# Attention scores of a hybrid decoder layer: two maps of a head by pairs of 64-row matmuls

## The chip, the cores and the metric

The kernel runs on one core of one Trainium2 chip. A core has five engines that run side by side, each with its own queue of instructions: TensorE (PE, matrix products; PEld is its loading of the stationary operand), VectorE (DVE), ScalarE (ACT), GpSimd (POOL) and SyncE (SP, which here issues DMAs). Matrix products land in PSUM, a small memory of 128 partitions in banks of 512 float32 values; everything else lies in SBUF, also with 128 partitions. The metric is device time in microseconds for one execution, lower is better. All times are of the kernel as a whole unless a stretch is named.

## What is computed

One decoder layer on 1024 tokens of width 1024, batch 1, in float32. One RMS norm feeds one input projection. Its columns go to two groups of heads that mix the tokens in parallel: four heads of differential attention, and four heads of a gated delta rule (a chunked recurrence). The outputs are joined, projected, added to the input, and followed by an MLP with squared ReLU (hidden width 4096). The part that the change touches is the attention:

```python
da_q = rms_norm(da_q.reshape(B, S, DA_HEADS, 2, DA_QK_DIM), q_norm_w[l])   # 4 heads, 2 maps, 64 dims
da_k = rms_norm(da_k.reshape(B, S, DA_HEADS, 2, DA_QK_DIM), k_norm_w[l])
...
s = jnp.einsum('bqhcd,bkhcd->bhcqk', qb, k, preferred_element_type=jnp.float32) * scale
s = jnp.where(causal, s, jnp.finfo(jnp.float32).min)
p = jax.nn.softmax(s, axis=-1)
a = p[:, :, 0] - lam * p[:, :, 1]
return jnp.einsum('bhqk,bkhe->bqhe', a.astype(v.dtype), v)
```

For each head there are two maps. Each map has queries and keys of 64 dimensions; the two softmax maps are subtracted with a learned factor and the difference is applied to values of 128 dimensions.

## The kernel before

**Precision.** Products that need more than one rounded operand are made with the type fp32r: a float32 matrix is split into a high part (rounded to fp32r) and a low part (the rest), and the products high·high, high·low and low·high are added up in PSUM. The projections do so with three matmuls for each block of 128 (lines 1089 to 1091 for the attention's projection, 267 to 269 for the delta rule's, 1389 to 1391 for the output projection).

**Queries and keys.** `da_units` projects blocks of 256 columns (two heads of two maps) for each of eight blocks of 128 tokens, and normalises them. `da_turns` transposes such a block with two matmuls against the identity (lines 1050 and 1051), writes high and low part into the tile `qa` of `[128, 2, 256]` (lines 1054 and 1055), and stores it in device memory as `qk_d`. On the host the columns of the units of q and k are reordered before the launch (map before head), so that one transposed block of 128 rows holds one map of two heads.

**Scores.** `scores` walks through 32 units: a head h and a block of 128 queries tb. The unit looks at n = 128·(tb+1) keys. Where n is over 512, the keys are cut into two pieces of pl = n/2, because a matmul writes at most one bank. `load_head` brings the keys of a head: for each of the two maps a tile `KS0` or `KS1` with the 64 dimensions of the high part in the upper half of the partitions and those of the low part in the lower half. `load_q` brings the queries of a unit twice: in `qa` as high over low, in `qb` as low over high. A matmul of all 128 rows with `qa` gives high·high + low·low, one with `qb` gives low·high + high·low (lines 1216 and 1217). So a map takes two matmuls for each piece, and a unit four or eight.

**Softmax.** A map's scores lie in one PSUM tile of two banks. One instruction on VectorE (line 1227) negates the scores, adds the causal mask, writes them to SBUF as `pexp`, and keeps the row minimum; ScalarE then takes the exponential with that minimum as bias and sums the rows (line 1228). When both maps are done, VectorE combines them (lines 1236 to 1239).

**Values.** `values` transposes the combined map (line 1261), copies it (line 1263), multiplies it with the values (line 1273), normalises the result and stores it or keeps it for the output projection.

**Order of the work.** A planner, the class `Interleave`, runs generators (`scan`, `da_units`, `da_turns`, `scores`, `values`, `mixed`, `outproj`) and decides in which order their matmuls stand in TensorE's one queue. Each generator says when it may go on; `flow.pe` advances the planner's clock by an estimate of PE time, `flow.chain` estimates when the other engines will have finished, and `flow.hold` keeps a PSUM buffer taken until then. For scores there are two PSUM buffers, `qsc` and `rsc`, which take turns once the delta rule's scan has been emitted. The estimates decide the order; on the chip the engines wait for semaphores. The instructions of the other engines are put in order by the framework's own scheduler. SP's queue carries the loads of `KS`, of the queries, of weights and of rows for the output projection.

Of the kernel before, what the change touches and what calls it, by code (L numbers as in the profile page):

```python
# [9 lines left out]
F32 = mybir.dt.float32  # L10
F32R = mybir.dt.float32r
BF16 = mybir.dt.bfloat16
AF = mybir.ActivationFunctionType
ALU = mybir.AluOpType
# [4 lines left out]
P = 128  # L19
SEQ = 1024  # L20
DM = 1024
KB = DM // P
NT = SEQ // P
HEADS = 4
DQK = 64
# [84 lines left out]
def act(n, accum=False):  # L110
    return "S", 55.0 + 0.83 * n + (93.0 if accum else 0.0)


def vec(n, extra=0.0):
    return "V", 68.0 + 1.045 * n + extra
# [7 lines left out]
def tile_hymba_layer(  # L123
# [6 lines left out]
    nc = tc.nc  # L130
    V, S, G, T = nc.vector, nc.scalar, nc.gpsimd, nc.tensor
# [45 lines left out]
    qk_d = dram.tile([2, 2, NT, P, 2, 2 * P], F32, name="qk_d")  # L177
# [85 lines left out]
    quarters, newest = Quarters(), {}  # L263
# [219 lines left out]
    with tc.manual_schedule(engines={T.engine, V.engine, S.engine, G.engine}):  # L483
# [38 lines left out]
        pools = {3: (pj, "pj"), 4: (ph, "ph"), 5: (pt_, "pt"), 6: (pj, "pj"), 7: (ph, "ph")}  # L522
# [10 lines left out]
        for tb in range(3, NT):  # L533
            for u in range(2):
                nxt, at = spread_at.get((tb, u), (None, 0))
                z[tb, u] = z_mm(tb, u, *pools[tb], nxt, at)
                if nxt is not None:
# [4 lines left out]
                    if nxt in (4, 5):  # L542
                        b = {4: 5, 5: 7}[nxt]
# [73 lines left out]
    u, au, e, w1, lw, d1, z1 = (n32(n) for n in ("gu", "gau", "gte", "gw1", "glw", "gd1", "gz1"))  # L617
# [128 lines left out]
    for h in range(HEADS):  # L746
        for hf in range(2):
            rh, rl = ta("rrh", 1, F32R), ta("rrl", 1, F32R)
            for t, col in ((rh, ggh), (rl, ggl)):
                for c in range(4):  # L750
                    i = cidx(h, 4 * hf + c)
# [26 lines left out]
    for h, hf, y, th in skew(dn_proj(1)):  # L778
# [6 lines left out]
        for c in range(4):  # L785
            i = cidx(h, 4 * hf + c)
# [9 lines left out]
        for c in range(4):  # L796
            i = cidx(h, 4 * hf + c)
            cs = slice(c * P, (c + 1) * P)
# [52 lines left out]
    for h, hf, q2 in skew(dn_proj(0)):  # L851
# [6 lines left out]
        for c in range(4):  # L858
            i = cidx(h, 4 * hf + c)
# [3 lines left out]
        for c in range(4):  # L863
            i = cidx(h, 4 * hf + c)
            cs = slice(c * P, (c + 1) * P)
# [26 lines left out]
    ae = actx.enter_context(tc.tile_pool(name="ae", bufs=4, **right))  # L892
    dctx = ctx.enter_context(ExitStack())
    ap = dctx.enter_context(tc.tile_pool(name="ap", bufs=1, **right))
# [6 lines left out]
    flow = Interleave()  # L901
    MK = 512 + P
    mk = ap.tile([P, MK], BF16, name="mk")
# [7 lines left out]
    pools, T_ops = {}, []  # L911
# [222 lines left out]
    def load_head(h, pool):  # L1134

        KS = []
        for m in range(2):
            k = pool.tile([P, SEQ], F32R, tag=f"KS{m}", name=f"KS{m}")
            for s in range(2):
                nc.sync.dma_start(k[HF[s]].bitcast(F32).rearrange("p (b t) -> p b t", t=P),  # L1140
                                  qk_d[h // 2, 1, :, HF[h % 2], s, m * P:(m + 1) * P].rearrange("b p t -> p b t"))
            KS.append(k)
        return KS

# [3 lines left out]
        return vt  # L1148

    def load_q(h, tb):  # L1150
        qa = ap.tile([P, 2, P], F32R, tag="qa", name="qa", bufs=2)
        qb = ap.tile([P, 2, P], F32R, tag="qb", name="qb", bufs=2)
        for s in range(2):
            src = qk_d[h // 2, 0, tb, HF[h % 2], s, :]
            nc.sync.dma_start(qa[HF[s]].bitcast(F32).rearrange("p m t -> p (m t)"), src)
            newest["SP"] = nc.sync.dma_start(qb[HF[1 - s]].bitcast(F32).rearrange("p m t -> p (m t)"), src)
        return qa, qb

    order = [(0, t) for t in range(NT)] + [(1, t) for t in range(NT)]
    order += [(h, t) for t in reversed(range(NT)) for h in (2, 3)]  # L1160
# [2 lines left out]
    def scores():  # L1163
        heads, npe, nsc = {}, 0, 0
        while state["da"] < 1:
            yield flow.now + 300, None
        yield flow.now + HEAD_T, None
        heads[0] = load_head(0, ap), load_v(0, ap)
        q = load_q(*order[0])
        yield flow.now + 6000, None  # L1170
        for u, (h, tb) in enumerate(order):
            if u >= NT - 3 and 1 not in heads and state["scan"] or h == 1 and 1 not in heads:

                while not state["scan"]:
                    yield flow.now + 300, None
                with tc.issue_after(newest["SP"].ins):
                    heads[1] = load_head(1, pools["a2"]), load_v(1, pools["a2"])
                if h == 1:
                    yield flow.now + 5000, None
            if h == 2 and h not in heads:  # L1180
                while state["turned"] < 3 * NT:
                    yield flow.now + 300, None
                ks = load_head(2, ap), load_head(3, pools["a2"])
                while state["da"] < 2:
                    yield flow.now + 300, None
                q = load_q(h, tb)
                heads[2] = ks[0], load_v(2, ap)
                heads[3] = ks[1], load_v(3, pools["a2"])
                yield state["da_t"] + 2000, None
            if q is None:  # L1190
                q = load_q(h, tb)
                yield flow.now + 3000, None
            while u < 2 * NT and u > 2 + 0.4 * (state["units"] - 3 * NT) and not state["proj"]:

                yield flow.now + 100, None
            while len(ready) > (AHEAD if state["scan"] else 0):
                yield flow.now + 100, None
            KS, vt = heads[h]
            qa, qb = q
            n = (tb + 1) * P  # L1200
            npc = 1 if n <= 512 else 2
            pl = n // npc
            pe, ssum = [], ap.tile([P, 2], F32, tag="ssum", name="ssum", bufs=4)
            mx = ap.tile([P, 2], F32, tag="mx", name="mx", bufs=4)
            for m in range(2):
                nsc += 1
                if state["scan"] and nsc % 2:
                    name, sc = "rsc", pools["rsc"]
                else:
                    name, sc = "qsc", qsc  # L1210
                yield 0, name
                sc = sc.tile([P, 1024], F32, tag="sc", name="ps_sc")
                for pc in range(npc):
                    o = sc[:, 512 * pc:512 * pc + pl]
                    ks = KS[m][:, pc * pl:(pc + 1) * pl]
                    T.matmul(o, qa[:, m, :], ks, start=True, stop=False)
                    T.matmul(o, qb[:, m, :], ks, start=False, stop=True)
                npe += 1
                ep = pools["be"] if state["scan"] and npe % 3 == 0 else ae
                e = ep.tile([P, SEQ], F32, tag="pexp", name="pexp")  # L1220

                scv, ev, mv = sc[:, :n], e[:, :n], mk[:, MK - n:]
                if npc == 2:
                    scv = sc.rearrange("p (a b) -> p a b", b=512)[:, :, :pl]
                    ev = ev.rearrange("p (a b) -> p a b", a=2)
                    mv = bass.AP(mk.tensor, mk.offset, [[MK, P], [MK - pl, 2], [1, pl]])
                V.tensor_tensor_reduce(ev, scv, mv, -1.0, 3.0e38, ALU.add, ALU.min, mx[:, m:m + 1])  # L1227
                S.activation(e[:, :n], e[:, :n], AF.Exp, scale=-1.0, bias=mx[:, m:m + 1],  # L1228
                             accum_out=ssum[:, m:m + 1])
                flow.pe(2 * max(n / 2.4, 110.0))  # L1230
                t = flow.chain(vec(n, 60))
                flow.hold(name, t)
                t = flow.chain(act(n, True), start=t - flow.HOP)
                pe.append(e)
            ri = ap.tile([P, 2], F32, tag="ri", name="ri", bufs=4)
            V.reciprocal(ri, ssum)
            cf = ap.tile([P, 1], F32, tag="cf", name="cf", bufs=4)
            V.scalar_tensor_tensor(cf, ssum[:, 0:1], nlam, ri[:, 1:2], ALU.mult, ALU.mult)
            V.scalar_tensor_tensor(pe[0][:, :n], pe[1][:, :n], cf, pe[0][:, :n], ALU.mult, ALU.add)
            t = flow.chain(vec(10), vec(1, 60), vec(n, 100), start=t - flow.HOP)  # L1240
            if u + 1 < len(order) and order[u + 1][0] // 2 < state["da"]:
                q = load_q(*order[u + 1])
            ready.append((h, tb, pe[0], ri, vt, t))
# [685 lines left out]
def _laid_out(_np, inputs):  # L1929


    w_in, w_out = (_np.asarray(inputs.pop(n))[0].reshape(KB, P, -1).transpose(1, 0, 2) for n in ("w_in", "w_out"))
    w_z = _np.zeros((2, KB // 2, P, 576), w_in.dtype)
    w_z[..., :2 * UC] = w_in[:, :, 3072:].reshape(P, KB // 2, 2, 2, UC).transpose(3, 1, 0, 2, 4).reshape(
        2, KB // 2, P, 2 * UC)
    units = w_in[:, :, :3072].reshape(P, KB, 12, 256).transpose(2, 0, 1, 3).copy()

    units[:4] = units[:4].reshape(4, P, KB, 2, 2, DQK).transpose(0, 1, 2, 4, 3, 5).reshape(4, P, KB, 256)
    halves = w_out.reshape(P, KB, 2, 512).transpose(2, 0, 1, 3)

    x_cols = _np.asarray(inputs["x"])[0].reshape(NT, P, KB, P).transpose(0, 3, 2, 1)
    w1_cols = _np.asarray(inputs.pop("norm1_w"))[0].reshape(KB, P).T
    return dict(inputs, x_cols=x_cols, w1_cols=w1_cols, w_z=w_z, w_units=units, w_halves=halves)
# [24 lines left out]
```

## Time and profile before

| what | value |
|---|---|
| median of 3 runs | 1227.69 us (1225.83 to 1229.32) |
| the profiled execution's own time | 1227.74 us |
| its span | 1226.0 us |
| granted TensorE clock, mean | 0.998 |
| instructions | 18798 |
| PE matmuls | 6743 |
| score matmuls (lines 1216 and 1217) | 192, from 359.5 to 571.3 us |
| DMA packets | 179269, 202.12 MB |

How to read the profile: a line such as `L1216 PE MATMUL ps_sc<-KS,qa 128*128 128x512 f32 x24` names the line of the kernel, the engine, the operation, output and inputs by the program's names, the stationary operand's rows times columns, the size of the moving one, and how many there were. A duration of a matmul includes the pipeline through the array, which overlaps the next matmul; the distance between two starts shows what a matmul costs in a row of them. In the waits view a line reads: who waited, for whom, microseconds in total, times, longest. In the windows view the columns are the stretch, its length, the busy time of PE, PEld, DVE, ACT and POOL with their numbers of instructions, the granted clock, the share of DMA, and GB/s. SPq is the queue in which SP issues DMAs.

### The profile page before, as it was taken

How to read it: one execution, taken by the hardware profiler on the slowest of the kernel's cores; microseconds unless marked ns; L12 is line 12 of the kernel's file. 1: busy time of each engine (PE TensorE's matmuls, PEld its weight loads, DVE VectorE, ACT ScalarE, POOL GpSimd, SP SyncE). 2: the span in 40 equal slices, each digit the busy share in tenths (PEclk: the TensorE clock that was granted, in tenths of full speed). 3: DMA queues.
4: the chain of work that ended last, by engine and by line, in shares of the span. 5: the costliest groups of instructions: out<-in, count | busy, mean ns of one | idle time of the engine just before them, and what ended most of it. 6: DMA issues, size and time to landing. Idle time of an engine off the chain costs nothing.

```text
span 1226.0 us, 18798 instructions
## 1 busy us (share of the span) xinstructions
PE 1208.2 (99%) x6743; PEld 1045.9 (85%) x6743; DVE 836.9 (68%) x1566; ACT 624.0 (51%) x1257; POOL 151.9 (12%) x215
## 2 busy tenths in 40 slices
PE   9999999999998999999999999999999999999998
PEld 7978888899998998888888888888888888888886
DVE  6868797667567667677798554566569755777543
ACT  6588554344355665566766444454563333333330
POOL 2411110035334431002200000000000000000000
PEclk9999999999999999999999999999999999999999
DMA  9334654378748865333628433444479555422301
GB/s 349 105 113 119 169 163 81 84 233 234 249 145 265 244 157 144 79 83 93 204 88 292 155 125 141 165 177 150 154 258 403 214 180 186 150 103 103 137 35 69
DMA packets 179269, 202.12 MB, mean 165 GB/s; under 512 B 63032, under 2 KB 135272, under 8 KB 179176
## 3 DMA queue, kind: packets, MB, share of 16 engines
q1 hardware_dynamic: 174552, 187.28, 48.0%
q0 software_dynamic: 4480, 13.64, 3.0%
q8 instruction: 53, 0.87, 0.3%
q14 instruction: 40, 0.33, 0.1%
q10 hardware_dynamic: 144, 0.00, 0.0%
HBM read 135.86 MB, written 65.01 MB: 164 GB/s over the span
## 4 chain that ended last, share of the span: by engine, by line
PE 91%; ACT 3%; DVE 2%; DMA 2%; SPq 1%; issue 1%; POOL 0%; DVEq 0%; ACTq 0%
PE X L1567 5%; PE X L1565 5%; PE X L1566 5%; PE X L1864 4%; PE X L1863 4%; PE X L1865 4%; PE ps_dn L267 3%; PE ps_qk L1089 3%; PE ps_dn L269 3%; PE ps_dn L268 3%; PE ps_qk L1090 3%; PE ps_qk L1091 3%; PE Y L1567 3%; PE Y L1565 3%; PE Y L1566 3%; PE ps_o L1273 3%
## 5 line engine op out<-in xcount | busy, mean ns | idle before, releaser
L1483 ACT CAST hH<-ur 128x1024 fp32r<-128x1024 f32 x56 | 58.9, 1051 | 173.3 <-PE Y L1864 90.3
L1484 DVE TENSOR_TENSOR hL<-ur,hH 128x1024 fp32r<-128x1024 f32 x56 | 68.4, 1223 | 79.8 <-ACT hH L1483 79.6
L1089 PE MATMUL ps_qk<-wH,hH 128*128 128x256 f32 x384 | 114.5, 298 | 0.7 <-DVE sn L1110 0.7
L1484 DVE TENSOR_TENSOR op<-raw,op 128x1024 fp32r<-128x1024 f32 x48 | 58.7, 1224 | 74.7 <-PE X L1566 40.7
L1090 PE MATMUL ps_qk<-wL,hH 128*128 128x256 f32 x384 | 108.7, 283 | 0.0
L1091 PE MATMUL ps_qk<-wH,hL 128*128 128x256 f32 x384 | 108.6, 283 | 0.0
L1863 PE MATMUL X<-hH 128*128 128x512 f32 x224 | 87.1, 389 | 0.0
L1864 PE MATMUL X<-hL,hH 128*128 128x512 f32 x224 | 87.1, 389 | 0.0
L1865 PE MATMUL X<-hH,hL 128*128 128x512 f32 x224 | 87.1, 389 | 0.0
L267 PE MATMUL ps_dn<-hH,wH 128*128 128x512 f32 x192 | 76.0, 396 | 0.2 <-ACT cp L683 0.2
L268 PE MATMUL ps_dn<-hL,wH 128*128 128x512 f32 x192 | 75.8, 395 | 0.0
L269 PE MATMUL ps_dn<-hH,wL 128*128 128x512 f32 x192 | 75.5, 394 | 0.0
L1089 PEld LDWEIGHTS ps_qk<-wH,hH 128*128 128x128 f32 x384 | 73.6, 192 | 1.4 <-DVE sn L1110 1.1
L1090 PEld LDWEIGHTS ps_qk<-wL,hH 128*128 128x128 f32 x384 | 73.7, 192 | 0.2
L1091 PEld LDWEIGHTS ps_qk<-wH,hL 128*128 128x128 f32 x384 | 73.4, 191 | 0.0
L1484 DVE TENSOR_TENSOR hL<-dw,hH 128x1024 fp32r<-128x1024 f32 x56 | 68.1, 1219 | 0.4 <-ACT hH L1483 0.4
L1483 ACT CAST op<-raw 128x1024 fp32r<-128x1024 f32 x48 | 50.4, 1051 | 35.1 <-PE Y L1567 19.9
L1483 ACT CAST hH<-dw 128x1024 fp32r<-128x1024 f32 x56 | 58.7, 1048 | 10.1 <-DMA dw<-in_w_down_dram 4.4
L1228 ACT ACTIVATE pexp<-pexp,mx 128x128 f32<-128x128 f32 (+7 forms) x64 | 49.6, 775 | 19.6 <-DVE mx L1227 18.7
L687 DVE SCALAR_TENSOR_TENSOR cy<-cp,pv,cy 128x512 f32<-128x512 f32 x72 | 53.7, 747 | 8.1 <-ACT cy L685 7.2
L1389 PE MATMUL ps_op<-wH,hH 128*128 128x512 f32 x128 | 53.3, 416 | 0.0
L1391 PE MATMUL ps_op<-wH,hL 128*128 128x512 f32 x128 | 50.3, 393 | 0.0
(380 smaller groups left out, 3428.7 us busy)
## 6 DMA issues: line engine op xcount, KB each, us to landing
ur<-ud SPq DMA_DIRECT2D x28, 1024.0 KB, 4.9
raw<-in_w_up_dram SPq DMA_DIRECT2D x32, 512.0 KB, 4.0
dw<-in_w_down_dram SPq DMA_DIRECT2D x32, 512.0 KB, 6.6
wraw<-in_w_units_dram SPq DMA_DIRECT2D x48, 256.0 KB, 3.7
qk_d<-qa POOLq DMA_DIRECT2D x32, 256.0 KB, 4.1
ud<-ua SPq DMA_DIRECT2D x16, 512.0 KB, 4.2
ud<-s SPq DMA_DIRECT2D x16, 512.0 KB, 2.6
pka<-park_d SPq DMA_DIRECT2D x32, 192.0 KB, 4.0
```

The lines of the kernel that those rows point to most:

```text
L267: T.matmul(ps, lh(k), rh(k), start=(k == 0), stop=False)
L268: T.matmul(ps, lh(k), rl(k), start=False, stop=False)
L269: T.matmul(ps, ll(k), rh(k), start=False, stop=(k == n - 1))
L1089: T.matmul(ps[:, :256], hH[:, k, sl], wh[:, k, :], start=(k == 0), stop=False)
L1090: T.matmul(ps[:, :256], hH[:, k, sl], wl[:, k, :], start=False, stop=False)
L1091: T.matmul(ps[:, :256], hL[:, k, sl], wh[:, k, :], start=False, stop=(k == KB - 1))
L1483: S.copy(dst[0], src)
L1484: V.tensor_tensor(dst[1], src, dst[0].bitcast(F32), ALU.subtract)
L1565: T.matmul(ps, op[0][:, k, cs], h[0][:, k, :], start=start and k == 0, stop=False, skip_group_check=True)
L1863: T.matmul(bank[t], v[0][:, j, sl], v[2][:, j], start=s0, stop=False, skip_group_check=True)
L1864: T.matmul(bank[t], v[0][:, j, sl], v[3][:, j], start=False, stop=False, skip_group_check=True)
L1865: T.matmul(bank[t], v[1][:, j, sl], v[2][:, j], start=False, stop=s1, skip_group_check=True)
```

## The change

The host's reordering of the columns goes, so a transposed block of 128 rows now holds both maps of one head, the first map in partitions 0 to 63 and the second in 64 to 127. `load_head` brings a tile of high parts and a tile of low parts, each with both maps; `load_q` brings one tile, with high and low part side by side. A matmul takes 64 rows: map m lies in the half `HF[m]` of the rows. For each piece of keys three products (high·high, low·high, high·low) are made for both maps in turn, six matmuls of 64 rows; each map writes its own bank of one PSUM tile. The minimum on VectorE is taken for each piece and map, the second piece starting from the minimum of the first; the exponentials follow once all pieces are there. The product low·low, which was made along, is no longer made. The planner's estimate for a piece is three matmuls of its width. The tile of queries has three buffers instead of two.

```diff
--- before.py
+++ after.py
@@ -1134,11 +1134,11 @@
     def load_head(h, pool):
 
         KS = []
-        for m in range(2):
-            k = pool.tile([P, SEQ], F32R, tag=f"KS{m}", name=f"KS{m}")
-            for s in range(2):
-                nc.sync.dma_start(k[HF[s]].bitcast(F32).rearrange("p (b t) -> p b t", t=P),
-                                  qk_d[h // 2, 1, :, HF[h % 2], s, m * P:(m + 1) * P].rearrange("b p t -> p b t"))
+        hs = slice(h % 2 * P, h % 2 * P + P)
+        for s in range(2):
+            k = pool.tile([P, SEQ], F32R, tag=f"KS{s}", name=f"KS{s}")
+            nc.sync.dma_start(k.bitcast(F32).rearrange("p (b t) -> p b t", t=P),
+                              qk_d[h // 2, 1, :, :, s, hs].rearrange("b p t -> p b t"))
             KS.append(k)
         return KS
 
@@ -1148,13 +1148,9 @@
         return vt
 
     def load_q(h, tb):
-        qa = ap.tile([P, 2, P], F32R, tag="qa", name="qa", bufs=2)
-        qb = ap.tile([P, 2, P], F32R, tag="qb", name="qb", bufs=2)
-        for s in range(2):
-            src = qk_d[h // 2, 0, tb, HF[h % 2], s, :]
-            nc.sync.dma_start(qa[HF[s]].bitcast(F32).rearrange("p m t -> p (m t)"), src)
-            newest["SP"] = nc.sync.dma_start(qb[HF[1 - s]].bitcast(F32).rearrange("p m t -> p (m t)"), src)
-        return qa, qb
+        qa = ap.tile([P, 2, P], F32R, tag="qa", name="qa", bufs=3)
+        newest["SP"] = nc.sync.dma_start(qa.bitcast(F32), qk_d[h // 2, 0, tb, :, :, h % 2 * P:h % 2 * P + P])
+        return qa
 
     order = [(0, t) for t in range(NT)] + [(1, t) for t in range(NT)]
     order += [(h, t) for t in reversed(range(NT)) for h in (2, 3)]
@@ -1196,42 +1192,38 @@
             while len(ready) > (AHEAD if state["scan"] else 0):
                 yield flow.now + 100, None
             KS, vt = heads[h]
-            qa, qb = q
             n = (tb + 1) * P
             npc = 1 if n <= 512 else 2
             pl = n // npc
             pe, ssum = [], ap.tile([P, 2], F32, tag="ssum", name="ssum", bufs=4)
-            mx = ap.tile([P, 2], F32, tag="mx", name="mx", bufs=4)
-            for m in range(2):
+            mx = ap.tile([P, 2, 2], F32, tag="mx", name="mx", bufs=4)
+            for pc in range(npc):
                 nsc += 1
                 if state["scan"] and nsc % 2:
                     name, sc = "rsc", pools["rsc"]
                 else:
                     name, sc = "qsc", qsc
                 yield 0, name
-                sc = sc.tile([P, 1024], F32, tag="sc", name="ps_sc")
-                for pc in range(npc):
-                    o = sc[:, 512 * pc:512 * pc + pl]
-                    ks = KS[m][:, pc * pl:(pc + 1) * pl]
-                    T.matmul(o, qa[:, m, :], ks, start=True, stop=False)
-                    T.matmul(o, qb[:, m, :], ks, start=False, stop=True)
-                npe += 1
-                ep = pools["be"] if state["scan"] and npe % 3 == 0 else ae
-                e = ep.tile([P, SEQ], F32, tag="pexp", name="pexp")
-
-                scv, ev, mv = sc[:, :n], e[:, :n], mk[:, MK - n:]
-                if npc == 2:
-                    scv = sc.rearrange("p (a b) -> p a b", b=512)[:, :, :pl]
-                    ev = ev.rearrange("p (a b) -> p a b", a=2)
-                    mv = bass.AP(mk.tensor, mk.offset, [[MK, P], [MK - pl, 2], [1, pl]])
-                V.tensor_tensor_reduce(ev, scv, mv, -1.0, 3.0e38, ALU.add, ALU.min, mx[:, m:m + 1])
-                S.activation(e[:, :n], e[:, :n], AF.Exp, scale=-1.0, bias=mx[:, m:m + 1],
-                             accum_out=ssum[:, m:m + 1])
-                flow.pe(2 * max(n / 2.4, 110.0))
-                t = flow.chain(vec(n, 60))
+                sc = sc.tile([P, 2, 512], F32, tag="sc", name="ps_sc")
+                cs = slice(pc * pl, pc * pl + pl)
+                for i, (a, b) in enumerate(((0, 0), (1, 0), (0, 1))):
+                    for m in range(2):
+                        T.matmul(sc[:, m, :pl], q[HF[m], a, :], KS[b][HF[m], cs], start=i == 0, stop=i == 2)
+                flow.pe(3 * max(pl / 2.4, 110.0))
+                c0 = 0 if pc + 1 < npc else MK - pl
+                for m in range(2):
+                    if pc == 0:
+                        npe += 1
+                        ep = pools["be"] if state["scan"] and npe % 3 == 0 else ae
+                        pe.append(ep.tile([P, SEQ], F32, tag="pexp", name="pexp"))
+                    V.tensor_tensor_reduce(pe[m][:, cs], sc[:, m, :pl], mk[:, c0:c0 + pl], -1.0,
+                                           mx[:, 0, m:m + 1] if pc else 3.0e38, ALU.add, ALU.min, mx[:, pc, m:m + 1])
+                t = flow.chain(vec(pl, 60), vec(pl, 60))
                 flow.hold(name, t)
-                t = flow.chain(act(n, True), start=t - flow.HOP)
-                pe.append(e)
+            for m in range(2):
+                e = pe[m][:, :n]
+                S.activation(e, e, AF.Exp, scale=-1.0, bias=mx[:, npc - 1, m:m + 1], accum_out=ssum[:, m:m + 1])
+            t = flow.chain(act(n, True), act(n, True), start=t - flow.HOP)
             ri = ap.tile([P, 2], F32, tag="ri", name="ri", bufs=4)
             V.reciprocal(ri, ssum)
             cf = ap.tile([P, 1], F32, tag="cf", name="cf", bufs=4)
@@ -1934,8 +1926,6 @@
     w_z[..., :2 * UC] = w_in[:, :, 3072:].reshape(P, KB // 2, 2, 2, UC).transpose(3, 1, 0, 2, 4).reshape(
         2, KB // 2, P, 2 * UC)
     units = w_in[:, :, :3072].reshape(P, KB, 12, 256).transpose(2, 0, 1, 3).copy()
-
-    units[:4] = units[:4].reshape(4, P, KB, 2, 2, DQK).transpose(0, 1, 2, 4, 3, 5).reshape(4, P, KB, 256)
     halves = w_out.reshape(P, KB, 2, 512).transpose(2, 0, 1, 3)
 
     x_cols = _np.asarray(inputs["x"])[0].reshape(NT, P, KB, P).transpose(0, 3, 2, 1)
```

## Prediction

> **What bounds the kernel now.** I read the page first (share of each engine, chain that ended last), then the stretch in which this code runs.
>
> ```profile
> span 1226.0 us, 18798 instructions
> PE 1208.2 (99%) x6743; PEld 1045.9 (85%) x6743; DVE 836.9 (68%) x1566; ACT 624.0 (51%) x1257; POOL 151.9 (12%) x215
> ...
> PE 91%; ACT 3%; DVE 2%; DMA 2%; SPq 1%; issue 1%; POOL 0%; DVEq 0%; ACTq 0%
> ```
>
> TensorE is busy 99% of the span and carries 91% of the chain. So a microsecond of PE time taken out is a microsecond gained, if PE is not left waiting where it went. The tile view of the scores gives place and shapes, and the windows view what else is busy there:
>
> ```profile
> L1216 PE MATMUL ps_sc<-KS,qa x96: 221/363/481, 359.5 to 571.2; 128*128 128x384 f32 x24, 128*128 128x512 f32 x24, 128*128 128x320 f32 x16, 128*128 128x448 f32 x16
> ...
> 355.00:580.00 225.00, 218.50 (x1480) 200.07 (x1479) 161.88 (x473) 140.66 (x383) 59.10 (x90) 0.99 0.56 151
> ```
>
> PE, its loads, DVE, ACT and POOL are busy for 218.5, 200.1, 161.9, 140.7 and 59.1 of 225 us. PE is idle for 6.5 us. The waits of PE in that window:
>
> ```profile
> PE ps_o L1273 <- DVE qa L1055: 2.3, 1, 2.3
> PE ps_at L1261 <- ACT at L1263: 1.3, 2, 1.1
> PE ps_qkt L1050 <- DVE om L1291: 1.0, 1, 1.0
> PE ps_o L1273 <- ACT at L1263: 1.0, 1, 1.0
> ...
> PE ps_sc L1217 <- DMA qb<-qk_d: 0.2, 1, 0.2
> ```
>
> The score matmuls themselves wait for almost nothing (0.2 us for a load of q); the rest is work behind them, in single waits.
>
> **Step 1: what a score matmul costs.** A PE duration holds a pipeline that overlaps the next one, so I use the distances between starts:
>
> ```profile
> 359.70 0.27 PE L1216 MATMUL ps_sc<-KS,qa 128*128 128x128 f32 x1
> 359.81 0.28 PE L1217 MATMUL ps_sc<-KS,qb 128*128 128x128 f32 x1
> ...
> 362.13 0.28 PE L1216 MATMUL ps_sc<-KS,qa 128*128 128x256 f32 x1
> 362.25 0.28 PE L1217 MATMUL ps_sc<-KS,qb 128*128 128x256 f32 x1
> ...
> 522.49 1.72 PE L1273 MATMUL ps_o<-vt,at 128*128 128x128 f32 x14
> 523.97 0.42 PE L1216 MATMUL ps_sc<-KS,qa 128*128 128x384 f32 x1
> 524.23 0.34 PE L1217 MATMUL ps_sc<-KS,qb 128*128 128x384 f32 x1
> 524.40 0.34 PE L1216 MATMUL ps_sc<-KS,qa 128*128 128x384 f32 x1
> ...
> 524.75 0.31 PE L1216 MATMUL ps_sc<-KS,qa 128*128 128x320 f32 x1
> 524.90 0.30 PE L1217 MATMUL ps_sc<-KS,qb 128*128 128x320 f32 x1
> ...
> 525.33 0.39 PE L1389 MATMUL ps_op<-wH,hH 128*128 128x512 f32 x1
> 525.57 0.40 PE L1390 MATMUL ps_op<-wL,hH 128*128 128x512 f32 x1
> 525.80 0.39 PE L1391 MATMUL ps_op<-wH,hL 128*128 128x512 f32 x1
> ```
>
> Distances: 0.11 us for 128 columns, 0.12 for 256, 0.15 for 320, 0.17 for 384, 0.23 to 0.24 for 512; 448 lies between at 0.20. The L1216 row (half of the 192 matmuls; its 16 unlisted ones are 128 and 256 wide, 8 each) doubles to 16, 16, 32, 48, 32 and 48 matmuls of 128, 256, 320, 384, 448 and 512 columns: 1.8 + 1.9 + 4.8 + 8.2 + 6.4 + 11.3 = **34.4 us** of PE.
>
> Now each piece of keys takes four full-height matmuls (two for each map). Afterwards it takes six of half height, in three pairs. If the two of a pair run side by side, a pair costs what one matmul costs now and three quarters are left, 25.8 us: **−8.6 us**. No row of before shows two matmuls side by side; all score rows are 128*128. The other bounds are the rivals below. I take the full overlap because the halves are disjoint in rows, in operands and in the PSUM bank that they write (one bank for each map), so nothing that the trace shows as shared orders them, except the weight path.
>
> The Trainium skill speaks for this: "TensorE: Matmul & The Clock Gate", Part 3, says that matmuls on different row groups start some 4 ns apart and run concurrently. It adds that a weight load overlaps a running matmul only if the row groups differ; there this trace disagrees, since 384 columns at 0.17 us leave no room for an uncovered load of the same rows.
>
> **Step 2: entering and leaving the half-height form.** Before has matmuls in another array form, with 64 stationary columns. What entering it costs:
>
> ```profile
> 206.06 0.39 PE L268 MATMUL ps_dn<-hL,wH 128*128 128x512 f32 x1
> 206.29 1.52 PE L837 MATMUL ps_h<-W,pb 128*96 128x96 f32 x16
> 207.59 0.47 PE L269 MATMUL ps_dn<-hH,wL 128*128 128x512 f32 x1
> ...
> 212.24 0.39 PE L268 MATMUL ps_dn<-hL,wH 128*128 128x512 f32 x1
> 212.56 1.15 PE L837 MATMUL ps_h<-W,pb 128*64 128x64 f32 x16
> 213.63 0.50 PE L269 MATMUL ps_dn<-hH,wL 128*128 128x512 f32 x1
> 213.97 0.39 PE L267 MATMUL ps_dn<-hH,wH 128*128 128x512 f32 x1
> ```
>
> The 96-column group starts 0.23 us after its forerunner, the 64-column group 0.32 us: 0.09 us to enter. Leaving costs 0.11 us (213.63 to 213.97 is 0.34 instead of 0.23). Today's scores pay the same 0.09 us when they follow f32 work: 523.97 to 524.23 is 0.26 instead of 0.17. The order of instructions of both programs shows 43 unbroken runs of score matmuls now, 31 of them behind f32 work, and 41 in the changed kernel, 31 of which lead into full-height fp32r matmuls. Entry then goes from 31 × 0.09 to 41 × 0.09 (+0.9), exit from nothing to 31 × 0.11 (+3.4) if it is paid at all. Bounds: −2.8 us (entry free too) and +8.0 us (entry twice as dear, exit paid). I take **+3.0 us**, nearest to the 64-column rows.
>
> The Trainium skill speaks against the change here: "TensorEngine Tiling (Array Packing)", Key Properties, says that a change of tiling mode drains TensorE. By that rule every run drains twice, 82 times in all, an estimate of 8 us at 0.1 us each, and the gain of step 1 would be gone; the 64-column rows agree that there is a price.
>
> **Step 3: VectorE, ScalarE and the path of a unit.** The masked minimum (L1227) is cut into pieces:
>
> ```profile
> L1227 DVE CUSTOM_DVE_ANT_1 pexp<-ps_sc,mk 128x1024 f32<-128x1024 f32 x8 | 9.8, 1221 | 0.0
> L1227 DVE CUSTOM_DVE_ANT_0 pexp<-ps_sc,mk 128x512 f32<-128x512 f32 x8 | 5.5, 686 | 0.5 <-PE ps_sc L1217 0.5
> L1227 DVE DVE_READ_ACCUMULATOR2_ANT mx<- 128x1 f32 x64 | 5.4, 84 | 0.0
> ```
>
> Two pieces of 512 cost 2 × 686 + 84 − 1221 = 235 ns more than one of 1024. There are 16 units over 512 keys with two maps each: 32 × 0.235 = 7.5 us more for DVE, whose 161.9 of 225 us become some 169. That hides beside PE. What does not hide by itself is the path: the first exponential of a 1024-key unit now starts after 1221 + 84 ns, and afterwards after three pieces, 3 × 770 = 2310 ns, so its unit is ready 1.0 us later. The PE stream meanwhile has projection or output-projection matmuls; if their cover is gone, each such unit costs up to 1.0 us. ACT does the same exponentials.
>
> For the queues: SP issues four loads of q for a unit now and one afterwards, 96 issues fewer at 0.5 us, and 8 loads of keys instead of 16. PE waited 0.2 us for them, so this buys nothing directly. The reordering of w_in's columns falls away on the host. Every buffer of scores now holds both maps of a piece and is freed after two minima; no score matmul waits for DVE in the list above. For all this I take **+1.0 us**, between −3 (half of PE's 6.5 us of idling goes, q being there earlier) and +6.5 (it doubles).
>
> **Sum**: −8.6 + 3.0 + 1.0 = −4.6. The profiled execution took 1227.74 us beside its span of 1226.0, and the median is 1227.69, so the same number serves for both: **1223 us**.
>
> **Rivals.** *A: the weight loads set the pace.* These rows bear it out:
>
> ```profile
> 200.15 1.92 PE L829 MATMUL ps_p<-gb,lt 128*128 128x96 f32 x16
> 201.86 0.47 PE L268 MATMUL ps_dn<-hL,wH 128*128 128x512 f32 x1
> ```
>
> Sixteen matmuls of 96 moving columns with 128 stationary ones take 1.71 us, 0.107 each; the L837 group above, with 96 moving and 96 stationary columns, takes 1.30 us, 0.081 each. The stationary columns set the pace of narrow matmuls. If loads for the two halves go one after the other, a pair needs 0.22 us at least: 36 pieces up to 448 wide cost 0.66 and 12 of 512 cost 0.70, 32.2 us, −2.2 instead of −8.6. With the other two terms the time is 1229.5, no change. Against it: the halves' loads touch different rows. The Trainium skill ("TensorE: Matmul & The Clock Gate", LDWEIGHTS) says that a load of few rows takes as long as one of 128, which leaves this rival open.
>
> *B: the halves do not run side by side.* Six matmuls instead of four, each at today's distance: 1.5 × 34.4, +17.2, with the other terms **1249 us**, slower by 1.7%. It decides as soon as the second of a pair starts more than a third of a matmul's distance after the first, on average. For it: nothing in this trace shows overlap, and these are four-byte operands. Against it: the built program gives the two halves different places in the array. It would be a change that does not do what it says.
>
> *C: the longer path starves PE.* If the 16 long units each cost their 1.0 us, +16 instead of +1, the time is 1238. Against it: of PE's waits above only single ones reach 1 us.
>
> **How the numbers follow.** Forecast 0.50, A 0.25, B 0.20, C 0.05. 0.3% is 3.7 us, about what a measurement of this kernel can tell from no change: under 1224.0 is faster, over 1231.4 slower. Within the forecast, step 2's bounds spread it over 1217 to 1228: I give 0.37 faster, 0.10 same, 0.03 slower. A: 0.03, 0.12, 0.10. B and C are slower. Sums: 0.40 faster, 0.22 same, 0.38 slower. For the range, B's place at 1249 is left out (0.20); it goes from 1217 (step 2 near its lower bound) to 1238 (A with step 2's upper bound, and C). The likeliest case alone is 1217 to 1228.
>
> **What would show it.** In the changed profile: the two matmuls of a pair starting within some 0.02 us, pairs at 0.11 to 0.24 us by width (forecast), 0.22 at all widths (A), or single starts 0.11 to 0.24 apart (B). The first pair of a run 0.1 us late, and the fp32r matmul behind a run 0.1 us late (step 2). DVE up by 7 to 8 us. PE waits on L1253 and L1265 (the changed kernel's L1261 and L1273) near today's 4.6 us. I am wrong if pairs start apart, or if PE's idle time in this stretch moves by more than 5 us.

## The result, and the profile after

The changed kernel is slower: a median of 1239.11 us against 1228.51, a ratio of 1.0086 with a 95% interval of 1.0067 to 1.0106. Measured again beside the experiments below, it took 1235.98 us against 1228.43, a ratio of 1.0059 (1.0045 to 1.0073). In the first of these measurements the profiled execution was a disturbed one, with all of TensorE several times slower, so the profile read here is that of the second (pairs_again), whose span is 1234.5 us, 8.5 more than the 1226.0 of before.

The page first, busy time by engine and the chain:

```profile
span 1234.5 us, 18877 instructions
...
PE 1218.0 (99%) x6839; PEld 1039.3 (84%) x6839; DVE 844.2 (68%) x1630; ACT 621.4 (50%) x1257; POOL 152.9 (12%) x215
...
PE 88%; DVE 3%; DMA 3%; issue 2%; ACT 2%; POOL 1%; SPq 1%; DVEq 0%; ACTq 0%; POOLq 0%
```

PE is busy for 9.8 us more, with 96 more matmuls. It is not that PE waits: the windows view of the same stretch as before, and PE's waits in it:

```profile
355.00:580.00 225.00, 219.40 (x1538) 186.11 (x1537) 162.49 (x520) 132.93 (x363) 56.78 (x85) 0.98 0.46 130
```

```profile
PE ps_at L1253 <- DVE qa L1055: 2.8, 2, 2.5
PE ps_at L1253 <- ACT mx L1274: 1.6, 2, 1.4
PE ps_at L1253 <- DVE oft L292: 0.8, 1, 0.8
PE ps_o L1265 <- ACT at L1255: 0.2, 1, 0.2
```

PE is idle for 5.6 of 225 us (6.5 before), with 5.4 us of waits. So the matmuls themselves must cost more. The timeline of PE shows where. This is one piece of 384 keys between output-projection matmuls, as it stands in the queue:

```profile
523.78 0.40 PE L1383 MATMUL ps_op<-wH,hL 128*128 128x512 f32 x1
524.10 0.79 PE L1211 MATMUL ps_sc<-KS,qa 64*128 64x384 f32 x6
524.82 0.50 PE L1381 MATMUL ps_op<-wH,hH 128*128 128x512 f32 x1
525.16 0.40 PE L1382 MATMUL ps_op<-wL,hH 128*128 128x512 f32 x1
525.40 0.39 PE L1383 MATMUL ps_op<-wH,hL 128*128 128x512 f32 x1
```

Read the starts. From 523.78 to 524.10 are 0.32 us where a matmul of 512 columns takes 0.23 to 0.24 (525.16 to 525.40): 0.09 lost on entering. The six score matmuls then take 0.72 us. Six full-height ones would take 6 × 0.174 = 1.04 us, three of them 0.52: so the halves do run side by side, and 0.20 us are lost within the run. The next matmul takes 0.34 us instead of 0.23 (524.82 to 525.16): 0.11 lost on leaving. Together **0.40 us for one unbroken run** of 64-row matmuls, against a gain of one full-height matmul (0.174 us here).

The rows of the weight loads beside this piece show where the loss sits:

```profile
524.10 0.47 PEld L1211 LDWEIGHTS ps_sc<-KS,qa 64*128 64x128 f32 x6 [0.36 <-issue]
524.82 0.19 PEld L1381 LDWEIGHTS ps_op<-wH,hH 128*128 128x128 f32 x1 [0.25 <-issue]
524.93 0.19 PEld L1382 LDWEIGHTS ps_op<-wL,hH 128*128 128x128 f32 x1
525.16 0.19 PEld L1383 LDWEIGHTS ps_op<-wH,hL 128*128 128x128 f32 x1
```

The load for L1383 starts at 525.16, a whole matmul ahead of its own at 525.40. At the two borders the load starts only with its own matmul: at 524.10, after 0.36 us without a load, and at 524.82, after 0.25 us. The next load follows 0.11 us later (524.82 to 524.93). The timeline view merges equal neighbours; the single records of the trace say the same of the run. Its three pairs start at 524.10, 524.38 and 524.56, so the first one takes 0.28 us instead of 0.17. Each border thus costs 0.09 us in which nothing starts and 0.11 us for a load that nothing covers; of the 0.20 us inside the run, 0.11 lie at its start and 0.09 at its end. The two matmuls of a pair start 0.003 us apart (median of the 144 pairs).

Worked out in the same way for all runs of scores (distance to the next start, less the distance that this shape has in an undisturbed row), the price of a run is 0.39 us in the changed kernel and 0.025 in the kernel before. Where the 8.5 us of the profile come from:

| term | before | changed | difference |
|---|---|---|---|
| score matmuls at their undisturbed distances, us | 34.1 | 25.6 | −8.5 |
| entering and leaving, runs × price, us | 43 × 0.025 = 1.1 | 41 × 0.39 = 16.0 | +14.9 |
| PE idle, 355 to 580 us | 6.5 | 5.6 | −0.9 |

That makes +5.5. Some of the rest is the clock. The windows view for 355 to 410 us, first the kernel before, then the changed one (the number behind POOL is the granted clock):

```profile
355.00:410.00 55.00, 51.69 (x397) 50.29 (x396) 41.74 (x130) 35.20 (x93) 24.39 (x32) 0.97 0.77 226
```

```profile
355.00:410.00 55.00, 51.38 (x400) 46.60 (x399) 40.59 (x137) 33.06 (x90) 24.56 (x32) 0.94 0.71 220
```

6% of 55 us of PE time are lost to the clock instead of 3%, +1.7 us. Some 1.3 us of the 8.5 remain without a row of their own.

### The profile page after: what moved, and what is told of

It is laid out like the page before. It is cut to its first block, busy times and chain, and to the rows that moved or that the text cites. A ratio compares the mean times of both kernels' runs of the same rounds, so it can differ in the third digit from the quotient of the medians.

```text
span 6922.4 us, 18877 instructions
## 1 busy us (share of the span) xinstructions
PE 6915.6 (100%) x6839; PEld 5203.5 (75%) x6839; DVE 859.4 (12%) x1630; ACT 637.8 (9%) x1257; POOL 152.3 (2%) x215
## 4 chain that ended last, share of the span: by engine, by line
PE 100%; DVE 0%; DVEq 0%; ACT 0%; POOL 0%; issue 0%; POOLq 0%
PE X L1557 5%; PE X L1558 5%; PE X L1559 5%; PE X L1856 4%; PE X L1857 4%; PE X L1855 4%; PE ps_qk L1089 4%; PE ps_qk L1091 4%; PE ps_dn L267 4%; PE ps_dn L268 4%; PE ps_dn L269 4%; PE ps_qk L1090 4%; PE ps_o L1265 3%; PE ps_op L1381 3%; PE Y L1558 3%; PE Y L1557 3%
## 5 line engine op out<-in xcount | busy, mean ns | idle before, releaser
L1089 PE MATMUL ps_qk<-wH,hH 128*128 128x256 f32 x384 | 425.5, 1108 | 0.0
L1090 PE MATMUL ps_qk<-wL,hH 128*128 128x256 f32 x384 | 396.3, 1032 | 0.0
L1091 PE MATMUL ps_qk<-wH,hL 128*128 128x256 f32 x384 | 396.0, 1031 | 0.0
L1857 PE MATMUL X<-hH,hL 128*128 128x512 f32 x224 | 379.4, 1694 | 0.0
L1856 PE MATMUL X<-hL,hH 128*128 128x512 f32 x224 | 379.4, 1694 | 0.0
L1855 PE MATMUL X<-hH 128*128 128x512 f32 x224 | 379.2, 1693 | 0.0
L1089 PEld LDWEIGHTS ps_qk<-wH,hH 128*128 128x128 f32 x384 | 356.3, 928 | 16.7 <-issue 16.7
L1090 PEld LDWEIGHTS ps_qk<-wL,hH 128*128 128x128 f32 x384 | 361.6, 942 | 0.8 <-issue 0.8
L1091 PEld LDWEIGHTS ps_qk<-wH,hL 128*128 128x128 f32 x384 | 361.1, 940 | 0.0
L267 PE MATMUL ps_dn<-hH,wH 128*128 128x512 f32 x192 | 329.1, 1714 | 0.0
L269 PE MATMUL ps_dn<-hH,wL 128*128 128x512 f32 x192 | 326.5, 1702 | 0.0
L269 PEld LDWEIGHTS ps_dn<-hH,wL 128*128 128x128 f32 x192 | 174.9, 911 | 72.2 <-issue 71.4
```

Source lines behind the costliest of these rows:

```text
L267: T.matmul(ps, lh(k), rh(k), start=(k == 0), stop=False)
L269: T.matmul(ps, ll(k), rh(k), start=False, stop=(k == n - 1))
L1089: T.matmul(ps[:, :256], hH[:, k, sl], wh[:, k, :], start=(k == 0), stop=False)
L1090: T.matmul(ps[:, :256], hH[:, k, sl], wl[:, k, :], start=False, stop=False)
L1091: T.matmul(ps[:, :256], hL[:, k, sl], wh[:, k, :], start=False, stop=(k == KB - 1))
L1855: T.matmul(bank[t], v[0][:, j, sl], v[2][:, j], start=s0, stop=False, skip_group_check=True)
```

## The experiments

Two theories stand at the start: the pairs overlap and the loss lies in waits (1), or they do not overlap (2). The profile of pairs_again fits neither: overlap, and no more waiting than before. From the second group on, theory S is that each run of 64-row matmuls costs some 0.40 us whatever its length, and rival R that the cost lies with each pair.

**pairs_again**: the changed kernel, no edit.

> The changed kernel once more, for a profile of an ordinary execution. Theory 1 (the pairs overlap, the loss is in waits): the six matmuls of a piece of 512 span some 0.75 us, PE's busy time falls by several us and PE's idle time in the stretch of the scores rises from 6.5 us to over 15. Theory 2 (the pairs do not overlap, or little): starts about 0.2 us apart within a piece of 512, PE's idle time near 6.5 us, PE's busy time up by some 10 us. Time under both: 1.006 to 1.011 of before.

Measured: 1.0059 (1.0045 to 1.0073). Read above: a piece of 384 takes 0.72 us, PE's idle time did not rise, and its busy time rose by 9.8 us. Theory 1 is wrong on the waits, theory 2 on the overlap.

**full_by_piece**: before's matmuls in the changed order.

```diff
-            for m in range(2):            # a tile for each map, both pieces in it
+            for pc in range(npc):         # a tile for each piece, both maps in it
...
+                for m in range(2):
+                    T.matmul(sc[:, m, :pl], qa[:, m, :], KS[m][:, cs], start=True, stop=False)
+                    T.matmul(sc[:, m, :pl], qb[:, m, :], KS[m][:, cs], start=False, stop=True)
+                flow.pe(4 * max(pl / 2.4, 110.0))
```

> Before's layout, loads and four full-height matmuls for each piece, but with the changed kernel's order: both maps of a piece into one PSUM tile, the minimum for each piece and map, the exponentials at the end. Theory 1 (the longer path of a unit starves PE): slower than before by about as much as the change, 1.005 or more. Theory 2 (the 64-row matmuls cost it): within 0.3% of before.

Measured: 1236.66 us, 1.0063 (1.0050 to 1.0075). Taken by the time alone this would confirm theory 1. The waits view says that it is another loss:

```profile
PE ps_sc L1216 <- DMA qb<-qk_d: 4.9, 1, 4.9
PE ps_qk L1089 <- DVE sn L1110: 3.1, 4, 1.3
PE ps_sc L1215 <- DVE sn L1110: 1.7, 1, 1.7
```

PE's idle time between 340 and 660 us is 13.6 us here, 7.2 before and 7.0 in the changed kernel. The largest wait is for a load of `qb`, which the changed kernel does not make. So this run shows that the changed order together with the loads of before costs several microseconds of waits, and that the changed kernel, as built, does not pay them. It does not tell the theories apart.

**maps_in_turn**: the six matmuls of a piece map by map.

```diff
-                for i, (a, b) in enumerate(((0, 0), (1, 0), (0, 1))):
-                    for m in range(2):
+                for m in range(2):
+                    for i, (a, b) in enumerate(((0, 0), (1, 0), (0, 1))):
```

> The changed kernel with the six matmuls of a piece in another order: three of the first map, then three of the second, so that neighbours share their half of the rows and cannot overlap except where the maps meet. If pairs overlap in the changed kernel: PE's time for the scores rises from about 26 to 45 us or more, the time by 10 us or more over the changed kernel. If they do not: the same time as the changed kernel within 0.3%.

Measured: 1236.41 us, 1.0065 (1.0053 to 1.0078), the same as the changed kernel. By what was expected this would mean that nothing overlaps; the timeline says that everything still does:

```profile
523.52 0.40 PE L1383 MATMUL ps_op<-wH,hL 128*128 128x512 f32 x1
523.84 0.80 PE L1211 MATMUL ps_sc<-KS,qa 64*128 64x384 f32 x6
524.57 0.50 PE L1381 MATMUL ps_op<-wH,hH 128*128 128x512 f32 x1
```

The same piece takes 0.73 us (523.84 to 524.57), although the second map's first matmul now stands behind three of the first map. In the single records it starts 0.010 us after the first map's first, ahead of two matmuls that stand before it in the built program. So it need not stand beside its partner in the queue. My expectation had taken for granted that it must. Whether a 64-row matmul is simply twice as fast was open from here, and same_half answers it.

**pairs_plan4**: the planner told four matmul times for a piece.

```diff
-                flow.pe(3 * max(pl / 2.4, 110.0))
+                flow.pe(4 * max(pl / 2.4, 110.0))
```

> The changed kernel with the planner told four matmul times for a piece instead of three; nothing else. If the planner's order, built on too short an estimate, leaves PE waiting: 3 us or more faster than the changed kernel, with less PE idle time. If not: within 0.3% of it.

Measured: 1232.26 us, 1.0037 (1.0024 to 1.0050), 3.7 us faster than the changed kernel. The price of a run is the same (41 × 0.40), PE idles 4.6 us between 340 and 660 instead of 7.0, and in the windows view the clock for 355 to 410 us is 0.97 instead of 0.94. So the order that the planner finds is worth some microseconds, and the estimate that came with the change was not the best.

**merged**: both pieces of a unit in one run.

```diff
+            bufs = []
             for pc in range(npc):
                 nsc += 1
                 ...
+            for name, sc in bufs:
+                yield 0, name
+            for pc in range(npc):
+                name, sc = bufs[pc]
```

> The changed kernel, but a unit waits until both of its PSUM buffers are free and then issues the matmuls of both pieces in one go: 31 unbroken runs of 64-row matmuls instead of 41, the same 288 matmuls. Theory S (each run costs some 0.40 us for going into the 64-row form and out of it, whatever its length): 10 x 0.40 = 4 us faster than the changed kernel. Rival R (each pair costs some 0.1 us more than a full-height matmul, 144 pairs): no change against the changed kernel, beyond what waiting for two buffers costs.

Measured: 1234.78 us, 1.0057 (1.0043 to 1.0070), 1.2 us faster than the changed kernel and not 4; the spread of the times does not tell 1.2 us from nothing. The runs did what theory S says: 31 × 0.40 = 12.4 us instead of 16.0. But PE idles 10.0 us between 340 and 660 us instead of 7.0, which gives most of it back. A run of twelve:

```profile
475.63 0.38 PE L1257 MATMUL ps_at<-ident,pexp 128*128 128x128 f32 x2
475.94 1.67 PE L1215 MATMUL ps_sc<-KS,qa 64*128 64x512 f32 x12
477.55 1.60 PE L1269 MATMUL ps_o<-vt,at 128*128 128x128 f32 x12
```

1.61 us for six pairs at 0.23 are 1.38 + 0.23: the loss within a run is that of a run of six.

**merged_priced**: the same, with the planner told 15 ns more for each pair and 400 ns for each run.

```diff
-                flow.pe(3 * max(pl / 2.4, 110.0))
+                flow.pe(3 * max(pl / 2.4 + 15.0, 110.0) + (400.0 if pc == 0 else 0.0))
```

> As merged, with the planner told what the trace shows: 15 ns more for each pair and 400 ns for each run. Theory S: as merged, and up to 3 us faster where the planner's order then fits better; 1229 to 1231 us beside 1228.4 of before. Rival R: no change against the changed kernel.

Measured: 1236.98 us, 1.0067 (1.0054 to 1.0080): a miss. The runs cost 31 × 0.40 again, PE idles 10.1 us, and 6.8 us of the stretch ran at half clock. A better estimate of PE's time did not make a better order; the planner's results move by 4 to 5 us without a trend that I can name.

**half_extra** and **full_extra**: the kernel before, with one needless matmul for each unit; each run has one of the two added lines.

```diff
                 sc = sc.tile([P, 1024], F32, tag="sc", name="ps_sc")
+                if m == 0:
+                    T.matmul(sc[:, 0:P], qa[0:64, 0, :], KS[0][0:64, 0:P], start=True, stop=True)   # half_extra
+                    T.matmul(sc[:, 0:P], qa[:, 0, :], KS[0][:, 0:P], start=True, stop=True)         # full_extra
```

> The kernel before, with one needless matmul of 64 rows and 128 columns ahead of each unit's first score matmul, overwritten by it: 32 of them, so 32 times into the 64-row form and out. Theory S: 32 x (0.11 + 0.35 to 0.40) = 15 to 16 us slower than before. Rival R: 32 x 0.2 = 6 to 7 us slower.

> The kernel before, with the same needless matmul in full height (128 rows, 128 columns) at the same 32 places. Both theories: 32 x 0.11 = 3.5 us slower than before.

Measured: 1242.83 us (1.0119, 1.0102 to 1.0136) and 1232.17 us (1.0033, 1.0023 to 1.0044). The full-height one costs 3.6 us, as expected; the half-height one 14.3 us, near theory S and double what rival R allows. The difference of 10.7 us over 32 places is 0.33 us for once in and once out. The timeline of half_extra shows the same:

```profile
507.90 0.40 PE L1393 MATMUL ps_op<-wH,hL 128*128 128x512 f32 x1
508.22 0.32 PE L1214 MATMUL ps_sc<-KS,qa 64*128 64x128 f32 x1
508.48 0.47 PE L1218 MATMUL ps_sc<-KS,qa 128*128 128x448 f32 x1
508.78 0.36 PE L1219 MATMUL ps_sc<-KS,qb 128*128 128x448 f32 x1
```

0.09 us before it, 0.26 for a matmul that takes 0.11 in full height, and 0.30 instead of 0.20 behind it.

**same_half**: both maps on the upper half of the rows, so both are the first map.

```diff
-                        T.matmul(sc[:, m, :pl], q[HF[m], a, :], KS[b][HF[m], cs], start=i == 0, stop=i == 2)
+                        T.matmul(sc[:, m, :pl], q[HF[0], a, :], KS[b][HF[0], cs], start=i == 0, stop=i == 2)
```

> The changed kernel with all six matmuls of a piece on the upper half of the rows (the second map reads the first map's queries and keys, so both maps are the first). Theory O (two matmuls run side by side because they lie on different halves): nothing overlaps, PE's time for the scores goes from 25.6 to 51 us, the time to 1261 us, 1.027 of before. Rival F (a 64-row matmul is simply twice as fast as one of 128 rows): the same time as the changed kernel, 1.006 of before.

Measured: 1258.8 us, 1.0246 (1.0215 to 1.0278). The overlap comes from the halves. **one_pair** and **pairs_twice** make the first product alone, or all three twice; each has one of the two added lines, and the flag that closes the sum in PSUM moves to the last product:

```diff
-                for i, (a, b) in enumerate(((0, 0), (1, 0), (0, 1))):
+                for i, (a, b) in enumerate(((0, 0),)):                       # one_pair
+                for i, (a, b) in enumerate(((0, 0), (1, 0), (0, 1)) * 2):    # pairs_twice
```

> The changed kernel with only the first of the three products (high by high) for each piece; the two products with low parts are left out. Theory S (0.40 us for each of 41 runs, and a pair costs what a full-height matmul costs): 17.1 us less than the changed kernel, about 1219 us, 0.992 of before, and still some 16 us of transitions. Rival R (the cost lies with each pair): 17.1 + 96 x 0.11 = 27.7 us less, about 1208 us.

> The changed kernel with the three products of each piece made twice over in the same run, six pairs instead of three, so the scores are doubled. Theory S: 25.6 us more than the changed kernel, about 1261.5 us. Rival R: 25.6 + 144 x 0.11 = 41 us more, about 1277 us.

Measured: 1224.99 us (0.9970, 0.9954 to 0.9985) and 1265.05 us (1.0289, 1.0251 to 1.0326), 11.0 us less and 29.1 us more than the changed kernel. The times alone fit S only roughly (−17.1 and +25.6); PE's own time fits it closely. The timelines of one_pair, pairs_twice and same_half, one run of 384 columns each:

```profile
517.37 0.44 PE L1211 MATMUL ps_sc<-KS,qa 64*128 64x384 f32 x2
517.74 0.50 PE L1381 MATMUL ps_op<-wH,hH 128*128 128x512 f32 x1
```

```profile
547.31 1.31 PE L1211 MATMUL ps_sc<-KS,qa 64*128 64x384 f32 x12
548.55 0.50 PE L1381 MATMUL ps_op<-wH,hH 128*128 128x512 f32 x1
```

```profile
529.03 2.35 PE L1211 MATMUL ps_sc<-KS,qa 64*128 64x384 f32 x12
531.31 0.50 PE L1381 MATMUL ps_op<-wH,hH 128*128 128x512 f32 x1
```

One, three and six pairs of 384 columns take 0.37, 0.72 and 1.24 us from the first start to the next other matmul. That is a line: 0.174 us for each pair, the price of one full-height matmul, and 0.20 us for the run. With twelve on one half it is 2.28 us = 12 × 0.174 + 0.19, no overlap. The price of a run over all 41 is 0.40 us in one_pair and 0.40 in pairs_twice, so it does not depend on the number of pairs: rival R is out. What the times have beside this is waiting: PE idles 11.5 us between 340 and 660 us in one_pair (7.0 in the changed kernel, so 4.6 of the 17.1 us go back at once; some 1.5 us more have no row of their own), and 9.6 between 340 and 680 in pairs_twice, with 1.7 us more lost to the clock.

No version here that makes all three products beats the kernel before, and the numbers say why. By the measured distances, a piece gains one full-height matmul, 0.11 to 0.23 us by width, and a run costs 0.39. Two pieces of 512 in one run, the most that the two PSUM buffers hold, gain 0.46. With one run for each of the 16 two-piece units, and full-height matmuls for the rest, the gain would be 32 pieces at 0.147, 0.174, 0.200 and 0.229, 8 each = 6.0 us, and the price 16 × 0.39 = 6.2 us; that version was not run.

## Why the prediction was wrong

**Step 1, the pairs: right.** Forecast 34.4 to 25.8 us, −8.6; measured 34.1 to 25.6, −8.5, by the distances and by the line of one, three and six pairs. The two of a pair start 0.003 us apart, where the prediction asked for 0.02 at most.

**Step 2, entering and leaving: this is the step that failed.** It named the mechanism and sized it at +3.0 us, with bounds from −2.8 to +8.0; it measured +14.9. Two terms of it were wrong. First the price of a run. I read 0.09 us in and 0.11 us out from the rows around the 64-column matmuls and took those for the whole. They are the two outer parts, and the changed kernel shows them unchanged; 0.20 us more are lost inside the run. half_extra shows it too, 0.26 us for a matmul worth 0.11. The trace of before already held this part: in the single records of the 64-column group at 212.56 the starts lie 0.058 us apart, except 0.106 behind the first and 0.152 from the last to L269. That is 0.14 us lost inside, and with 0.09 before and 0.11 behind 0.34 us for one such group. The prediction did not look inside the group's 1.07 us. The weight loads of pairs_again show what makes up the price: 0.09 us and an uncovered load of 0.107 us (the L829 row of the prediction), twice, are 0.39. Why the load waits at a border, no row here shows; that the array must run empty first is a reading that fits. The Trainium skill's page "TensorEngine Tiling (Array Packing)", Key Properties, has the draining; it gives no figure for it, and my estimate of 8 us by that rule was half of what 41 runs cost.

Second, the credit. I took off 2.8 us because today's runs behind f32 work seemed to pay 0.09 us as well. They get it back: the last f32 matmul ahead of such a run is 0.08 us shorter than its neighbours (522.49 to 523.97 in the prediction's rows is 1.48 us for 14, where 14 × 0.111 are 1.55). Over both matmuls the price is 0.025 us a run. I had looked at one side of the border only. Besides, the terms given for the forecast, +0.9 and +3.4, add up to 4.3; the +3.0 that went into the sum has no row of its own.

**Step 3: within its bounds, but not of the sign that I took.** DVE is busy 7.3 us longer (forecast 7.5). PE's waits behind the scores are 5.4 us (4.6 before), and its idle time fell by 0.9 us, where I had set +1.0 for the longer path of a unit. In the experiments PE's idle time between 340 and 660 us lay 2.4 us below (pairs_plan4) to 4.6 us above (one_pair) that of the changed kernel, and 6.6 above it in full_by_piece, which makes other loads; such differences are as large as the bounds of −3 and +6.5. That 1.7 us would go to the clock stood in no step.

**The rivals.** A (weight loads one after the other) is out: a further pair of 384 would cost 0.22 us, and it costs 0.174. B (no overlap) is out by the starts of the pairs and by same_half, where the second of a pair starts 0.20 us after the first in the median. C (starving by the longer path) is not seen in the changed kernel. None of them had a fixed price for each run above 0.2 us, which is what decided. The forecast of 1223 us with −4.6 becomes +7.3 us with 14.9 in the place of 3.0, and the second measurement gives +7.5. The first gave +10.6; the 3 us between the two measurements have no cause on record.

## What to carry to other kernels

Splitting TensorE's rows doubled the rate of the 64-row products here, but going in and out cost 0.39 us, so it pays only if an unbroken run saves more than that: here at least three full-height matmuls of 384 columns. Count the runs in the order of instructions before counting the matmuls, and price a border over both of its sides and over the first and last instruction inside; the 64-column group of before held nearly the whole price, 0.34 us, for whoever read its matmuls one by one. Where a planner lays out the order, allow some microseconds either way for where the waits fall, and read the trace's distances, not the total time, to judge a change of this size.

## What the runs showed of the hardware that was not expected

- The partner of a pair need not be next in the queue: three matmuls of one half followed by three of the other took 0.73 us, as long as in alternation (0.72), and the second three began 0.010 us after the first. The Trainium skill, "TensorE: Matmul & The Clock Gate", Part 3, says that matmuls start in the order of the program; with that, this order could not have overlapped by more than the ends, so here the measurement decides against it.
- Weight loads for the two halves do not wait for each other: pairs of 384 columns follow one another at 0.174 us, less than two loads of 0.107, and in the single records of pairs_again the loads for the first pair both start at 524.10, those for the second both at 524.21.
- The price of a run does not depend on its length: 0.40 us with one pair to a piece and with six.
